# The order of seven products: TensorE's up-projection queue written by hand, and weight splits placed behind the operand turns

## The chip, the cores and the metric

The kernel runs on one core of a Trainium2 chip. The metric is the time of one execution in device microseconds (us). The core's engines work side by side, each on its own queue in order: TensorE (PE, matmuls; its weight loads are listed as PEld), VectorE (DVE), ScalarE (ACT), GpSimd (POOL), and SyncE (SP), which issues the DMAs.

## The reference

A hybrid encoder layer of width 1024 runs over a prompt of 512 tokens and a sample of 1024 tokens with shared weights. What matters here is its second half, for the sample:

```python
for l in range(DEPTH):                       # DEPTH = 1
    ...                                      # attention and convolution heads, added to x
    h = _rmsnorm(x, norm_ffn_g[l])
    u = _dwconv(h @ w_up[l], ffn_dw_w[l], ffn_dw_b[l])        # 3 taps along the tokens
    x = x + (jax.nn.silu(u[..., :D_FF]) * u[..., D_FF:]) @ w_down[l]
return _rmsnorm(x, norm_final_g)
```

`w_up` is 1024 x 5632 (a gate half and a value half of 2816 columns each), `w_down` 2816 x 1024. All numbers are 32-bit floats.

## The kernel before

**Precision.** A 32-bit operand is split into a high part that TensorE takes in its rounded 32-bit form and a low part, the rest. A product is then three matmuls: high by high, high by low, low by high (lines 1045 to 1047 of `prod`). A split is one copy on ACT (line 1031 or 970) and one subtraction on POOL or DVE (line 921, the helper `sub`; `add` is line 918).

**Stages.** The program first does projections, convolution and attention for both inputs, then the prompt's feed-forward half. From about 900 us on it does the sample's feed-forward half: the up-projection until about 1356 us and the down-projection to the end.

**The sample's up-projection.** It uses a Strassen-like scheme: a 2 x 2 block product with seven block products instead of eight. `NJ` = 22 blocks of 128 gate and 128 value columns (index `j`) are worked through, the two halves of 512 tokens side by side in a bank pair (left and right, `L` and `R`). Each block has seven products, numbered 1 to 7, each of four slices `c` by three matmuls of 128 x 128 by 128 x 512, so 84 matmuls. `A[i, c]` holds the activations' operand of product `i`, which lasts over all blocks; `ops[j, i]` holds the split weight operand of block `j`. `block_up` names quarters of a block's raw weights; `sums_up(j)` makes the weight sums that products 7, 6, 4, 5 need (one on POOL, three on DVE), and `split_up(j, i, ...)` splits the named operands. Products 1 and 2 take the raw quarters, so their splits come before the sums.

A block has two pairs of accumulator banks: `x` (gate) and `wy` (value), taken together by `pair_banks` from four such pairs. So two blocks can be under way. The products share banks:

```python
def first(j):                 # 1: into x left, then ACT copies it to wy right as a seed
    if j < NJ:
        pair_banks(j)
        s = st[j]
        prod(s["x"][:, L], j, 1, True, True)
        nc.scalar.copy(s["wy"][:, R], s["x"][:, L])          # line 1117
```

The others follow the same pattern: `second` adds product 2 to `x` left. `sixth` adds product 6 to `wy` right, and ACT copies the sum out (line 1126). `seventh` adds product 7 to `wy` right, and ACT copies the sum to `x` right as a seed (line 1135). `fourth` adds product 4 to `x` right. `fifth` puts product 5 into `wy` left, ACT copies it out (line 1146) and DVE adds it to `wy` right. `third` adds product 3 to `wy` left, and DVE adds the sum copied out by `sixth`. A product that adds to a seeded bank waits for the copy that seeds it.

`gate_part(j)` reads `x` out (ACT line 1158, two DVE taps, lines 1159 and 1160, then a tanh), `value_part(j)` does the same with `wy`, multiplies both (DVE lines 1177 and 1179) and writes to memory what the down-projection needs. Only then are the bank pairs free for block `j + 2`.

**Operand turns.** The activations' operands are rows that are scaled and summed (`scaled`, line 943, and `last_sum`), then turned by TensorE: `turned(i, get)` does four steps, each of four 128 x 128 transposes into one bank (line 968), an ACT copy and a DVE subtraction (lines 970 and 971). The last five operands (4, 6, 7, 5, 3; 20 steps) are turned during the products 2 and 4 of block 0 and 2 of block 1: `every(n, gen)` spreads n steps over the four slices of a product. The turn banks (four) are then given up, and their place becomes two more bank pairs. For blocks 0 and 1 the first products were made before these pairs exist; `armed` (line 1110) writes a dummy product into `wy` right so that later products may add to it, and ACT copies the first product over it (line 1243).

**Who orders the work.** A scheduler that simulates the engines places each instruction: those written first come first, but an engine that would be idle takes whatever is ready. Buffers are named slots (`Slots`), taken in the order in which they came free: 61 of 2048 bytes (`h`), two slightly larger (`d`), 15 of 4096 (`q`) and 4 of 4224 (`c`). `split_up` takes one `q` or `c` for both parts of an operand. `reserve` and `raws` set some `q` slots aside for raw weights (`load_up`, line 995). Inside `tc.manual_schedule(engines={...})` the named engines keep the written order. Before the change this holds for PE from the operand turns through the first blocks, and for SP from the last block on; in the loop over `j` the scheduler orders PE.

The loop body before, from line 1467 on:

```python
        split_up(j + 1, 1, 2)
        sixth(j)
        sums_up(j + 1)
        value_part(j - 1)
        second(j)
        seventh(j)
        split_up(j + 1, 6, 4)
        fifth(j)
        fourth(j)
        gate_part(j)
        ...                          # j == NJ - 1: SP by hand, load_next(10), down_step(0)
        first(j + 1)
        third(j)
        split_up(j + 1, 7, 5, 3)
```

**The down-projection** is again seven products, each over 11 pairs of blocks; `down_step(k)` is one step of 12 matmuls (lines 1346 to 1348). Its first step stands in the loop's last round.

Of the kernel before, what the change touches and what calls it, by code (L numbers as in the profile page):

```python
# [28 lines left out]
NJ = FF // P  # L29
# [67 lines left out]
def tile_hybrid_encoder(ctx: ExitStack, tc: tile.TileContext, xs, rel_bias, norm_attn_g, w_in,  # L97
# [819 lines left out]
    def add(out, a, b, eng=None):  # L917
        (eng or nc.vector).tensor_tensor(out, a, b, op=ALU.add)  # L918

    def sub(out, a, b, eng=None):  # L920
        (eng or nc.vector).tensor_tensor(out, a, b, op=ALU.subtract)  # L921
# [42 lines left out]
    def turned(i, get):  # L964
        for c in range(4):
            held, ap = get()
            for b in range(4):
                nc.tensor.transpose(ap[:, b * P:(b + 1) * P], block_rows(i, b)[:, c * P:(c + 1) * P], ident[:])
            hi, lo = A[i, c] = (sb.tile([NT], F32R), sb.tile([NT], F32R))
            nc.scalar.copy(hi[:], ap)  # L970
            sub(lo[:], ap, hi[:].bitcast(F32))
            held = None
            yield 0.0
        key = {6: "s2", 5: "s1", 7: 1, 3: 0}.get(i)
        for b in range(4):
            rows.pop((key, b), None)
# [9 lines left out]
    def reserve(n):  # L986
        for slot in [s for s in sb.free if s[0][0] == "q"][:n]:
            sb.free.remove(slot)
            raws.free.append(slot)

    def load_up(j, half):
        if j < NJ:
            r = uraw[j, half] = raws.tile([KC, P])
            col = half * FF + j * P
            nc.sync.dma_start(r[:], w_up[0][:, col:col + P].rearrange("(k p) c -> p k c", p=P))

    def block_up(j, half, k):
        return uraw[j, half][:, 4 * k:4 * k + 4, :].rearrange("p k c -> p (k c)")
# [8 lines left out]
    def sums_up(j):  # L1007
        if j < NJ:
            g0, g1, v0, v1 = (block_up(j, half, k) for half in range(2) for k in range(2))
            t = third_sum[j] = sb.tile([NT])  # L1010
            sub(t[:], v1, v0, nc.gpsimd)
            sub(v0, v0, g0)
            sub(g0, v1, v0)
            sub(g1, g1, g0)

    def split_up(j, *which, apart=False):
        if j >= NJ:
            return
        for i in which:
            if i == 7:  # L1020
                held = third_sum.pop(j)
                src = held[:]
            else:
                src = block_up(j, *{1: (0, 0), 2: (0, 1), 6: (0, 0), 4: (0, 1), 5: (1, 0), 3: (1, 1)}[i])
            if not apart and any(s[0][0] in "qc" for s in sb.free):
                t = sb.tile([2, NT], F32R)
                hi, lo = Part(t, 0), Part(t, 1)
            else:
                hi, lo = sb.tile([NT], F32R), sb.tile([NT], F32R)
            ops[j, i] = hi, lo  # L1030
            nc.scalar.copy(hi[:], src)  # L1031
            sub(lo[:], src, hi[:].bitcast(F32), nc.gpsimd)
            held = None
            done.add((j, i))
        for half, pair in ((0, (6, 4)), (1, (5, 3))):
            if (j, half) in uraw and all((j, i) in done for i in pair):
                uraw.pop((j, half))

    def prod(out, j, i, start, stop, between=None):
        whi, wlo = ops.pop((j, i))  # L1040
        go = dict(skip_group_check=not start)
        for c in range(4):
            hi, lo = A[i, c]
            s = slice(c * P, (c + 1) * P)
            nc.tensor.matmul(out, whi[:, s], hi[:], start=(start and c == 0), stop=False, **go)  # L1045
            nc.tensor.matmul(out, whi[:, s], lo[:], start=False, stop=False, **go)  # L1046
            nc.tensor.matmul(out, wlo[:, s], hi[:], start=False, stop=(stop and c == 3), **go)  # L1047
            if j == NJ - 1:
                A.pop((i, c))
            if between is not None:  # L1050
                next(between, None)
# [52 lines left out]
    def pair_banks(j):  # L1104
        st[j] = dict(x=wide(), wy=wide())

    def armed(out):

        hi, lo = A[1, 0]
        nc.tensor.matmul(out, hi[:, 0:P], hi[:], start=True, stop=True)  # L1110

    def first(j):
# [4 lines that stand above are left out]
            nc.scalar.copy(s["wy"][:, R], s["x"][:, L])  # L1117

    def second(j, between=None):
        prod(st[j]["x"][:, L], j, 2, False, True, between)  # L1120

    def sixth(j, between=None):
        s = st[j]
        s["u2"] = sb.tile([NT])
        prod(s["wy"][:, R], j, 6, False, True, between)
        nc.scalar.copy(s["u2"][:], s["wy"][:, R])

    def fourth(j, between=None, start=False):
        prod(st[j]["x"][:, R], j, 4, start, True, between)
# [11 lines left out]
    def fifth(j):  # L1141
        s = st[j]
        W, Y = s["wy"][:, L], s["wy"][:, R]
        prod(W, j, 5, True, True)
        p5 = sb.tile([NT])
        nc.scalar.copy(p5[:], W)
        add(Y, Y, p5[:])

    def third(j):
        s = st[j]  # L1150
        W = s["wy"][:, L]
        prod(W, j, 3, False, True)
        add(W, W, s.pop("u2")[:])
# [17 lines left out]
    def value_part(j):  # L1171
        if j < 0:
            return
        p = j // 2
        s = st.pop(j)
        ug, t = s["ug"], s["t"]
        nc.vector.scalar_tensor_tensor(t[:], t[:], 1.0, ug[:], op0=ALU.add, op1=ALU.mult)
        uv = dwconv(s.pop("wy"), NJ + j)
        nc.vector.tensor_tensor(t[:], t[:], uv[:], op=ALU.mult)
        del ug, uv  # L1180
        s.clear()
        if j % 2 == 0:
            even[p] = t
            nc.sync.dma_start(ga[1, p][:], t[:, L])
            return
        e, x, y = even.pop(p), sb.tile([W2]), sb.tile([NT])
        for i, blk in ((2, L), (4, R)):
            nc.sync.dma_start(ga[i, p][:], t[:, blk])
        add(x[:, R], e[:, R], t[:, R])
        sub(x[:, L], e[:, L], e[:, R], nc.gpsimd)  # L1190
        sub(e[:, R], x[:, R], e[:, L])
        sub(y[:], t[:, L], e[:, R], nc.gpsimd)
        for i, b in ((5, x[:, R]), (7, x[:, L]), (6, e[:, R]), (3, y[:])):
            nc.sync.dma_start(ga[i, p][:], b)
# [3 lines left out]
    by_hand = tc.manual_schedule(engines={mybir.EngineType.PE})  # L1198
# [6 lines left out]
    def chain(*gens):  # L1205
        for g in gens:
            yield from g

    def every(n, gen):

        for c in range(4):
            for _ in range((n * (c + 1)) // 4 - (n * c) // 4):
                next(gen, None)
            yield

    turns = chain(*(turned(i, turn_bank) for i in (4, 6, 7, 5, 3)))
# [5 lines left out]
        nc.scalar.copy(a[:], st[j]["x"][:, L])  # L1222
        firsts.append(a)
    second(0, every(7, turns))
    split_up(0, 7)
    fourth(0, every(7, turns), True)
    split_up(1, 7)
    split_up(0, 5)
    second(1, every(6, turns))
    for _ in turns:  # L1230
        raise RuntimeError("turns left")
    pt_guard.__exit__(None, None, None)
# [6 lines left out]
    def arm():  # L1239
        for j in range(2):  # L1240
            Y = st[j]["wy"][:, R]
            armed(Y)
            nc.scalar.copy(Y, firsts[j][:])
            yield

    fourth(1, chain(iter((None,)), arm()), True)
    firsts.clear()
    reserve(2)
    load_up(2, 0)
    load_up(2, 1)  # L1250
    split_up(1, 5)
    sixth(0)
    split_up(0, 3)
# [10 lines left out]
    fifth(1)  # L1264
    sums_up(2)
    third(0)
    split_up(2, 6, 4)
    value_part(0)
    first(2)
    third(1)  # L1270
    split_up(2, 7, 5, 3)
    load_up(4, 0)
    load_up(4, 1)
    by_hand.__exit__(None, None, None)


    pr, second_half = {}, {}
# [181 lines left out]
    for j in range(2, NJ):  # L1459
        for half in range(2):  # L1460
            load_up(j + 3, half)
        if j >= NJ - 3:
            sb.free.extend(raws.free)
            raws.free.clear()
        if j >= NJ - 2:
            load_next(4)
        split_up(j + 1, 1, 2)
        sixth(j)
        sums_up(j + 1)
        value_part(j - 1)  # L1470
        second(j)
        seventh(j)
        split_up(j + 1, 6, 4)
        fifth(j)
        fourth(j)
        gate_part(j)
        if j == NJ - 1:
            by_hand = tc.manual_schedule(engines={mybir.EngineType.SP})
            by_hand.__enter__()
            load_next(10)  # L1480
            down_step(0)
        first(j + 1)
        third(j)
        split_up(j + 1, 7, 5, 3)
    sb.free.extend(raws.free)
    value_part(NJ - 1)

# [70 lines left out]
```

## Time and profile before

| What | us |
|---|---|
| Median of 3 runs (lowest to highest) | 1568.78 (1568.59 to 1568.99) |
| The profiled execution, its own time | 1569.84 |
| Its span, first to last instruction | 1568.1 |
| PE busy | 1523.8 (97% of the span) |
| DVE busy | 1161.2 (74%) |
| ACT busy | 797.8 (51%) |
| POOL busy | 786.9 (50%) |

A row of a timeline reads: start, length, engine, line, operation, output<-inputs by the program's names, shapes, count, and in brackets the idle time before it and what ended it. A row of the waits reads: who waits, for what, microseconds in total, times, longest. A row of groups reads: line, engine, operation, names, shapes, count, then busy time, mean nanoseconds of one, and idle time before. A row of stretches gives the length and then, for PE, weight loads, DVE, ACT and POOL, the busy time and count, then TensorE's granted clock, the DMA share and GB/s. Matmuls overlap, so their pace is read from their starts and not from their recorded lengths.

### The profile page before, as it was taken

The numbers are of one execution on the slowest core, as the hardware profiler recorded it, in microseconds if no ns is written. First come the engines' busy times: TensorE is split into PE (matmuls) and PEld (weight loads), VectorE is DVE, ScalarE is ACT, GpSimd is POOL, SyncE is SP. The second block draws the span as 40 slices with busy tenths as digits, with TensorE's granted clock in tenths as the row PEclk, the third lists the DMA queues.
The fourth block names the chain that finished last, engine by engine and source line by source line (L and its number), as shares of the span: only waits on it lengthen the run. The fifth ranks groups of instructions, "written<-read, shape, count | busy, mean of one in ns | idle before, by whom it ended". The sixth has DMA issues, their size and how long they took to land.

```text
span 1568.1 us, 20174 instructions
## 1 busy us (share of the span) xinstructions
PE 1523.8 (97%) x6909; PEld 1238.2 (79%) x6909; DVE 1161.2 (74%) x1687; ACT 797.8 (51%) x1426; POOL 786.9 (50%) x603
## 2 busy tenths in 40 slices
PE   8999999999998999999999999999999999999998
PEld 6787788887887778888877878777777778888886
DVE  7999868638988996756675858576766676877795
ACT  4634565335565655655554355454545445454364
POOL 7651344238575676656652337575757566000225
PEclk9999999999999999999999999999999999999999
DMA  7573246446332333333656222323232332594642
GB/s 228 158 199 95 86 120 162 128 138 164 108 115 62 107 108 108 107 96 98 213 182 198 81 68 78 110 93 109 88 114 89 108 101 98 176 383 149 221 142 108
DMA packets 209771, 207.62 MB, mean 132 GB/s; under 512 B 11156, under 2 KB 150748, under 8 KB 209541
## 3 DMA queue, kind: packets, MB, share of 16 engines
q1 hardware_dynamic: 209669, 206.35, 41.9%
q8 instruction: 54, 0.88, 0.2%
q14 instruction: 48, 0.39, 0.1%
HBM read 158.84 MB, written 48.51 MB: 132 GB/s over the span
## 4 chain that ended last, share of the span: by engine, by line
PE 77%; DVE 10%; DMA 4%; issue 3%; POOL 3%; ACT 2%; SPq 0%; POOLq 0%; ACTq 0%; DVEq 0%
PE w L1045 8%; PE w L1047 8%; PE w L1046 8%; PE w L1347 5%; PE w L1346 5%; PE w L1348 5%; PE u L250 4%; PE u L251 4%; PE u L253 4%; DVE c L293 3%; PE b L253 3%; PE b L250 3%; PE b L251 3%; PE u L641 2%; PE u L642 2%
## 5 line engine op out<-in xcount | busy, mean ns | idle before, releaser
L144 POOL TENSOR_TENSOR q<-q,q 128x1024 fp32r<-128x1024 f32 x72 | 174.9, 2434 | 70.1 <-ACT q L143 32.0
L1045 PE MATMUL w<-h,q 128*128 128x512 f32 x470 | 185.4, 396 | 4.6 <-ACT w L1135 2.6
L921 POOL TENSOR_TENSOR q<-q,q 128x512 fp32r<-128x512 f32 x101 | 143.1, 1429 | 91.8 <-ACT q L1031 91.7
L1047 PE MATMUL w<-h,q 128*128 128x512 f32 x470 | 184.4, 392 | 0.0
L1046 PE MATMUL w<-h,q 128*128 128x512 f32 x448 | 175.7, 392 | 0.0
L250 PE MATMUL u<-h,q 128*128 128x512 f32 x400 | 159.9, 400 | 3.6 <-DVE h L775 2.8
L251 PE MATMUL u<-h,q 128*128 128x512 f32 x400 | 159.5, 399 | 0.6 <-DVE h L212 0.6
L253 PE MATMUL u<-h,q 128*128 128x512 f32 x384 | 152.1, 396 | 2.1 <-POOL q L144 2.1
L293 DVE SCALAR_TENSOR_TENSOR c<-c,cvw,c 128x512 f32<-128x512 f32 x184 | 138.1, 750 | 2.4
L143 ACT CAST q<-q 128x1024 fp32r<-128x1024 f32 x72 | 75.6, 1049 | 78.8 <-POOL q L144 45.5
L1045 PEld LDWEIGHTS w<-h,q 128*128 128x128 f32 x470 | 88.2, 188 | 27.6 <-ACT w L1135 4.4
L1047 PEld LDWEIGHTS w<-h,q 128*128 128x128 f32 x470 | 88.2, 188 | 20.5
L250 PE MATMUL b<-h,q 128*128 128x512 f32 x256 | 102.1, 399 | 1.7 <-DVE d L323 1.7
L1346 PE MATMUL w<-h,h 128*128 128x512 f32 x264 | 103.6, 392 | 0.0
L1348 PE MATMUL w<-h,h 128*128 128x512 f32 x264 | 103.6, 392 | 0.0
L921 DVE TENSOR_TENSOR h<-h,h 128x512 fp32r<-128x512 f32 (+1 forms) x128 | 92.7, 766 | 11.4 <-ACT h L925 8.8
L251 PE MATMUL b<-h,q 128*128 128x512 f32 x256 | 100.6, 393 | 0.0
L253 PE MATMUL b<-h,q 128*128 128x512 f32 x256 | 100.6, 393 | 0.0
L1046 PEld LDWEIGHTS w<-h,q 128*128 128x128 f32 x448 | 84.1, 188 | 18.5
L918 POOL TENSOR_TENSOR q<-q,q 128x1024 f32<-128x1024 f32 x8 | 23.8, 2985 | 146.4 <-DVE q L918 135.6
L1347 PE MATMUL w<-h,h 128*128 128x512 f32 x244 | 95.9, 393 | 0.0
L250 PEld LDWEIGHTS u<-h,q 128*128 128x128 f32 x400 | 76.4, 191 | 20.8 <-DVE h L775 3.3
(452 smaller groups left out, 4099.3 us busy)
## 6 DMA issues: line engine op xcount, KB each, us to landing
q<-in_w_up SPq DMA_DIRECT2D x88, 512.0 KB
h<-in_w_down SPq DMA_DIRECT2D x90, 256.0 KB
ga<-q SPq DMA_DIRECT2D x64, 256.0 KB
h<-ga SPq DMA_DIRECT2D x57, 256.0 KB
q<-in_w_in SPq DMA_DIRECT2D x28, 512.0 KB
q<-in_x_sample SPq DMA_DIRECT2D x15, 512.0 KB
h<-qsd SPq DMA_DIRECT2D x24, 256.0 KB
q<-ga SPq DMA_DIRECT2D x20, 256.0 KB
```

What stands on the lines that cost most here:

```text
L144: (nc.vector if dve else nc.gpsimd).tensor_tensor(lo[:], raw[:], hi[:].bitcast(F32), op=ALU.subtract)
L250: nc.tensor.matmul(out, whi[:, kc, :], hi[:], start=(kc == 0), stop=False)
L251: nc.tensor.matmul(out, whi[:, kc, :], lo[:], start=False, stop=False)
L253: nc.tensor.matmul(out, wlo[:, kc, :], hi[:], start=False, stop=(kc == KC - 1))
L293: nc.vector.scalar_tensor_tensor(acc[:], src(t), w(t), acc[:], op0=ALU.mult, op1=ALU.add)
L921: (eng or nc.vector).tensor_tensor(out, a, b, op=ALU.subtract)
L1045: nc.tensor.matmul(out, whi[:, s], hi[:], start=(start and c == 0), stop=False, **go)
L1046: nc.tensor.matmul(out, whi[:, s], lo[:], start=False, stop=False, **go)
L1047: nc.tensor.matmul(out, wlo[:, s], hi[:], start=False, stop=(stop and c == 3), **go)
L1346: nc.tensor.matmul(out, sh[:, c], th[:], start=(p == 0), stop=False)
L1347: nc.tensor.matmul(out, sh[:, c], tl[:], start=False, stop=False)
L1348: nc.tensor.matmul(out, sl[:, c], th[:], start=False, stop=(p == NPAIR - 1))
```

## The change

PE's hand order no longer ends before the loop but covers the whole up-projection, and from the last block on a second one covers SP and PE to the end of the kernel. In the loop the products are written in another order: second, seventh, first of the next block, fifth, fourth, sixth of the next block, third. The splits of operands 7, 5 and 4 move to other places in the round. In the prologue the splits of operand 7 of blocks 0 and 1 and of operand 5 of block 0 stand behind the turns, the last turns are spread as eight steps over four slices, so they end one slice earlier, and the arming of the two banks comes one slice later.

```diff
@@ -1222,11 +1222,8 @@
     second(0, every(7, turns))
-    split_up(0, 7)
     fourth(0, every(7, turns), True)
-    split_up(1, 7)
-    split_up(0, 5)
-    second(1, every(6, turns))
+    second(1, chain(every(8, turns)))
     for _ in turns:
         raise RuntimeError("turns left")
@@ -1243,11 +1240,14 @@
-    fourth(1, chain(iter((None,)), arm()), True)
+    fourth(1, chain(iter((None, None)), arm()), True)
     firsts.clear()
+    split_up(0, 7)
+    split_up(1, 7)
     reserve(2)
     load_up(2, 0)
     load_up(2, 1)
+    split_up(0, 5)
     split_up(1, 5)
     sixth(0)
     split_up(0, 3)
@@ -1264,14 +1264,14 @@
     fifth(1)
     sums_up(2)
     third(0)
-    split_up(2, 6, 4)
+    split_up(2, 6)
     value_part(0)
     first(2)
     third(1)
-    split_up(2, 7, 5, 3)
+    split_up(2, 7, 5, 4, 3)
     load_up(4, 0)
     load_up(4, 1)
-    by_hand.__exit__(None, None, None)
+    sixth(2)
@@ -1465,23 +1465,26 @@
         split_up(j + 1, 1, 2)
-        sixth(j)
+        second(j)
         sums_up(j + 1)
         value_part(j - 1)
-        second(j)
         seventh(j)
-        split_up(j + 1, 6, 4)
+        split_up(j + 1, 6)
+        first(j + 1)
         fifth(j)
+        split_up(j + 1, 7, 5)
         fourth(j)
         gate_part(j)
-        if j == NJ - 1:
-            by_hand = tc.manual_schedule(engines={mybir.EngineType.SP})
+        if j < NJ - 1:
+            sixth(j + 1)
+        else:
+            by_hand.__exit__(None, None, None)
+            by_hand = tc.manual_schedule(engines={mybir.EngineType.SP, mybir.EngineType.PE})
             by_hand.__enter__()
             load_next(10)
             down_step(0)
-        first(j + 1)
         third(j)
-        split_up(j + 1, 7, 5, 3)
+        split_up(j + 1, 4, 3)
```

## The prediction

> **What bounds the kernel now.** I read the page's busy shares first, then TensorE's waits from 900 us on, then its timeline at each wait, and last the other engines' timelines beside them.
>
> ```profile
> PE 1523.8 (97%) x6909; PEld 1238.2 (79%) x6909; DVE 1161.2 (74%) x1687; ACT 797.8 (51%) x1426; POOL 786.9 (50%) x603
> PE w L1045 <- ACT w L1135: 2.6, 4, 0.7
> PE t L968 <- DVE h L921: 2.0, 1, 2.0
> PE w L1045 <- ACT w L1117: 1.9, 4, 0.5
> PE w L1110 <- DVE q L921: 1.4, 1, 1.4
> 1039.30:1118.50 79.20, 78.03 (x337) 62.91 (x336) 52.63 (x49) 38.50 (x57) 51.46 (x37) 1.00 0.31 100
> 1356.00:1568.10 212.10, 205.08 (x890) 166.78 (x889) 157.68 (x212) 97.85 (x178) 44.20 (x39) 0.99 0.57 195
> ```
>
> The first row says that TensorE (PE) is the bound. The next four are all that TensorE waited for between 900 and 1360 us, the stretch that the change touches: recorded idle time, times, longest. Nothing else there can be gained. The two last rows are stretches (length, then busy time of PE, weight loads, DVE, ACT, POOL, then clock): four blocks of the up-projection's loop, and the down-projection.
>
> What a wait costs is read from the starts of the matmuls, since their recorded ends overlap the next.
>
> ```profile
> 1045.05 0.40 PE L1045 MATMUL w<-h,q 128*128 128x512 f32 x1
> 1045.28 0.40 PE L1046 MATMUL w<-h,q 128*128 128x512 f32 x1
> 1045.52 0.40 PE L1047 MATMUL w<-h,q 128*128 128x512 f32 x1
> 1046.58 0.50 PE L1045 MATMUL w<-h,q 128*128 128x512 f32 x1 [0.66 <-ACT w L1135]
> 1046.91 0.39 PE L1046 MATMUL w<-h,q 128*128 128x512 f32 x1
> ```
>
> Undisturbed matmuls start 0.23 us apart, so a product of 12 takes 2.76 us and a block of 84 takes 19.3 us. Here one start comes after 1.06 us and the next after 0.33: 0.83 + 0.10 = 0.93 us lost, 0.27 more than the 0.66 recorded as idle. For the loop's eight waits that is 2.6 + 1.9 + 8 x 0.27 = 6.7 us. The stretch of four blocks agrees: 336 matmuls would take 77.3 of its 79.2 us, and the 1.9 us left over holds two waits.
>
> **The loop (6.7 us at stake).** Both waits are a product that sits too close behind the ACT copy which seeds its bank. At 1046.58 the fourth product comes straight after the seventh, whose sum ACT must first copy (L1135). In the other kind the sixth waits for the first product's copy (L1117), and that copy waits for something itself:
>
> ```profile
> L1117 ACT COPY w<-w x20: 570/570/590, 955.2 to 1323.3; 128x512 f32<-128x512 f32 x20
>   DVE q L1160: 11.1, 8
> L918 DVE TENSOR_TENSOR w<-w,h 128x512 f32<-128x512 f32 x39 | 27.2, 696 | 37.4 <-ACT h L1146 30.1 <-PE w L1047 7.3
> L1158 ACT ACTIVATE q<-w,vecs,fw 128x1024 f32<-128x1024 f32 x40 | 48.3, 1208 | 28.7 <-PE w L1047 25.3 <-DVE w L918 2.4 <-DMA ga<-q 0.6
> L1160 DVE SCALAR_TENSOR_TENSOR q<-w,fw,q 128x1023 f32<-128x1023 f32 x39 | 49.8, 1278 | 0.7
> L921 POOL TENSOR_TENSOR q<-q,q 128x512 fp32r<-128x512 f32 x89 | 125.4, 1422 | 68.7 <-ACT q L1031 68.7
> ```
>
> The second row, from the idle times of L1117, says what the copy waited for: the last depthwise tap of the value part two blocks back, which still reads the bank pair that the copy writes.
>
> In the new hand order each block runs second, seventh, first of the next block, fifth, fourth, sixth of the next block, third. Seventh to fourth, first to sixth and fifth to third then each have two other products between them: 5.5 us for a copy of 0.57. The long chain starts where the third product ends: DVE's add 0.70, ACT's 1.21, two taps of 1.28, together 4.5 us. The sixth of the next block starts five products later (second, seventh, first, fifth, fourth: 13.8 us), so after the copy some 8.7 us are left for what DVE has queued ahead: three sums and one 1024-wide operation, about 4 us by the 0.70 row and the 1.28 row. I count both kinds of wait gone.
>
> The operand splits lose cover. A split is a copy on ACT (0.57, as L1117's of the same size) and a subtraction of 1.42 on POOL. The next block's first operand is now written two products (5.5 us) ahead of its use, where it was five; two splits take 2 x 1.42 + 0.57 = 3.4 us, and they may run earlier than written, since the new order holds at most seven operand pairs at once where the old held eight, which leaves a slot more. Fourth's split moves behind the third product: it keeps the raw half-block a little longer, and the load into that place is needed two blocks (38 us) later, against a landing time like this one of an equal 512 KB load:
>
> ```profile
> 90.48 4.08 DMA q<-in_w_in
> ```
>
> So the loads cost nothing. If one split is late now and then I allow 0.5 us: 6.7 - 0.5 = 6.2 us gained.
>
> **The operand turns (3.9 us at stake).**
>
> ```profile
> 908.23 0.48 PE L1045 MATMUL w<-h,q 128*128 128x512 f32 x1
> 909.22 0.27 PE L968 MATMUL t<-ident,c 128*128 128x128 f32 x1
> 909.33 0.27 PE L968 MATMUL t<-ident,q 128*128 128x128 f32 x1
> 911.65 0.66 PE L968 MATMUL t<-ident,h 128*128 128x128 f32 x4 [2.04 <-DVE h L921]
> 917.94 0.48 PE L1045 MATMUL w<-h,h 128*128 128x512 f32 x1
> 919.51 0.48 PE L1045 MATMUL w<-h,h 128*128 128x512 f32 x1
> 912.00:914.00 2.00, 2.00 (x11) 1.72 (x10) 1.98 (x4) 0.59 (x1) 0.00 (x0) 0.66 0.00 0
> 914.00:916.00 2.00, 2.00 (x9) 1.60 (x8) 1.16 (x2) 1.17 (x2) 0.00 (x0) 0.50 0.04 8
> ```
>
> Three products and two turns take 1.57 us when nothing waits (917.94 to 919.51), and a turn of four transposes 0.11 apart is 0.43. From 908.23 to 917.94 lie twelve products and seven turns: 4 x 1.57 - 0.43 = 5.85 us, but 9.71 passed. Of the 3.9 us lost, 2.0 is the wait, and the rest the granted clock, which fell to 0.66 and 0.50 behind it (2 x 0.34 + 2 x 0.50 = 1.7 us).
>
> ```profile
> 897.55 1.40 DVE L943 SCALAR_TENSOR_TENSOR c<-q,rs,q 128x512 f32<-128x512 f32 x2
> 903.73 2.44 DVE L943 SCALAR_TENSOR_TENSOR q<-c,rs,q 128x512 f32<-128x512 f32 x2 [1.53 <-POOL rs L128]
> 907.55 1.77 DVE L921 TENSOR_TENSOR q<-q,q 128x512 f32<-128x512 f32 x1
> 909.36 1.63 DVE L921 TENSOR_TENSOR q<-q,h 128x512 f32<-128x512 f32 x1
> 910.91 3.07 DVE L921 TENSOR_TENSOR h<-t,h 128x512 fp32r<-128x512 f32 x5
> 904.23 1.40 POOL L921 TENSOR_TENSOR q<-h,q 128x512 fp32r<-128x512 f32 x1 [0.53 <-ACT q L1031]
> 906.99 1.78 POOL L921 TENSOR_TENSOR q<-h,q 128x512 fp32r<-128x512 f32 x1 [1.36 <-ACT q L1031]
> 908.73 1.71 POOL L921 TENSOR_TENSOR q<-q,q 128x512 fp32r<-128x512 f32 x1
> ```
>
> The transposes at 911.65 need a turn bank that DVE frees with its first subtraction at 910.91. DVE is late because its row sums run beside three POOL subtractions, which are the splits that the change moves: 2.44 instead of 1.40 for the pair, 1.77 and 1.63 instead of the 0.70 of the add's row, 3.0 us in all. Without them the subtraction starts near 907.9 and no transpose waits. Written behind the turns they could still run early, as ACT and POOL take what is ready. But the two third sums now hold their small slots through the turns, so the last turned operands overflow into the large slots that those splits had, and the splits are left with slots that come free only when a turned row is done. If only the third of the three moves away, 0.9 us is gained; if all, 3.9; if the moved splits meet another DVE sum of 0.70, up to 1 us comes back. I take 3.2, near the upper end, since the slots speak for it.
>
> [...]
>
> **The armed banks (1.6 us at stake).**
>
> ```profile
> 927.16 1.18 ACT L1031 CAST q<-q 128x512 fp32r<-128x512 f32 x2
> 928.20 0.62 ACT L970 CAST d<-t 128x512 fp32r<-128x512 f32 x1
> 927.86 0.40 PE L1047 MATMUL w<-h,h 128*128 128x512 f32 x1
> 929.61 0.50 PE L1110 MATMUL w<-h 128*128 128x512 f32 x1 [1.35 <-DVE q L921]
> 930.14 0.59 ACT L1243 COPY w<-h 128x512 f32<-128x512 f32 x1 [1.31 <-PE w L1110]
> ```
>
> The arming matmul writes where the turn banks lay and waits until the last turn is read out, whose ACT copy stands behind two splits. It starts 1.75 us after its forerunner instead of 0.23, and the next start is 0.1 late as before: 1.6 us lost. The change ends the turns three matmuls earlier in second(1) and arms three matmuls later in fourth(1): 6 x 0.23 = 1.4 us, so 0.2 remains, or nothing if the splits have left ACT. New is that the sixth follows the second arming matmul at once. The first bank's copy ends 930.73, 1.12 us after its arming matmul; the sixth starts five matmuls (1.15 us) after it: 0 to 0.1, or 0.6 with a split ahead on ACT. Net 1.4 us gained, between 0.8 and 1.6.
>
> **The down-projection.** Its order is now by hand too. The page shows no wait for TensorE in its 212 us, and 77 steps of 12 matmuls at 0.23 are 212.5 us, so an order cannot gain. It can lose at the seam, where the first down step comes behind fourth(21), one product of the loop before the end, and seventh(21) has only one product between itself and fourth(21), 2.76 us for a 0.57 copy: 0 to 0.5 us, taken as 0.2.
>
> **Sum.** 6.2 + 3.2 + 1.4 - 0.2 = 10.6 us of the profiled execution's 1569.8, so 1559.2. That execution is 1.1 us above the median of the runs, and the median becomes 1558.2. If everything is gained (6.7 + 3.9 + 1.6) it is 1556.6; with each stage's lower end (4 in the loop, 0.9, 0.8) and 0.5 lost at the seam 5.2 is gained: 1563.6. A measurement of this kernel can tell about 0.2%, 3.1 us, from no change. Chance of this case 0.64.
>
> **Rivals.** First, the loop's waits come back elsewhere: DVE and POOL are busy 52.6 and 51.5 of 79.2 us, so taps can finish late and the wait moves to another product of the hand order, at about its old size. Then only turns and arming gain, 4.4 us: 1564.4. Against it: each pair has 5.5 us. Chance 0.11.
>
> Second, the gain is given back: the down steps' operands are not ready sooner (DVE is busy 157.7 of 212 us), and TensorE waits there for what it has won. 1568.8 at worst. Against it: no wait is seen there, and the splits would have to be late at once. Chance 0.08.
>
> Third, slower: first of the next block waits for its operand in every block. If its split starts only with second(j), and POOL has two other subtractions ahead (2 x 1.42), the operand is ready 2 x 1.42 + 3.4 = 6.2 us later against 5.5, and with POOL slowed to 1.75 as beside DVE above 7.6: a wait of 0.7 to 2.1 us in each of 19 blocks, 13 to 40 us, less the 10.6: 1571 to 1598, for one number 1580. It decides from 0.56 us a block on, where the gain is eaten. A fixed order also cannot put another product into the hole, as a free one can. For it: POOL is busy in 65% of the loop. Against it: today no TensorE wait in the loop is for POOL, and one slot more is free. Chance 0.17.
>
> The range takes in the forecast's ends and the first two rivals, and a little of the third: 1556.0 to 1571.0, which leaves out most of the third and about 0.03 below. Faster by over 0.2% (below 1565.7): 0.64 and most of the first rival, 0.73. Within: 0.09. Slower: 0.18.
>
> **What would show it.** Right: the waits of TensorE hold neither L1135 nor L1117 in the loop, four blocks take about 77.4 us, the rows of DVE at 903 to 911 are 0.7 us each with no POOL subtraction beside them, the clock stays at 1.00 through the turns, and the arming matmul waits under 0.3 us. Wrong: a wait of TensorE for a POOL or ACT split (L921, L1031's result) once per block, POOL subtractions still beside the row sums, or a new wait in the down-projection's stretch.

## The result, and the profile after

The changed kernel takes 1630.32 us (median of 6 runs, 1626.43 to 1634.58), the kernel before 1568.16 us beside it. The ratio is 1.0399, with a 95% interval of 1.0378 to 1.0420: 62 us slower, where 10.6 us faster was forecast.

TensorE's waits in the changed kernel, from 890 us to the end (its span is 1629.8 us):

```profile
PE w L1045 <- ACT q L1031: 25.9, 8, 5.1
PE w L1047 <- POOL q L921: 21.6, 9, 3.7
PE w L1045 <- ACT w L1135: 0.9, 1, 0.9
```

The waits that the change was to remove are gone. Of the waits for seeding copies (L1117, L1135) one of 0.9 us is left, at the end of the loop. In their place stand 47.5 us of a kind that the kernel before did not have: a product waits for the high part of its weight operand (ACT's split, L1031) and then for the low part (POOL's subtraction, L921).

From one seventh product to the next both orders run one full block of products, so the first and last start of its copy (L1135) measure the loop. Before, and in the changed kernel:

```profile
L1135 ACT COPY w<-w x20: 570/570/582, 965.0 to 1341.0; 128x512 f32<-128x512 f32 x20
L1135 ACT COPY w<-w x20: 570/570/578, 959.2 to 1401.7; 128x512 f32<-128x512 f32 x20
```

The first is 5.8 us earlier and the last 60.7 us later: the preparation of blocks 0 and 1 gained, and the 19 blocks between took 442.5 us instead of 376.0. The preparation, as it was forecast (a stretch of the turns, then VectorE's and TensorE's timelines):

```profile
914.00:916.00 2.00, 2.00 (x16) 1.78 (x15) 1.70 (x3) 1.50 (x4) 0.13 (x1) 1.00 0.01 4
```

```profile
902.96 1.42 DVE L943 SCALAR_TENSOR_TENSOR q<-c,rs,q 128x512 f32<-128x512 f32 x2 [1.53 <-POOL rs L128]
905.75 0.68 DVE L921 TENSOR_TENSOR q<-q,q 128x512 f32<-128x512 f32 x1
924.36 0.50 PE L1110 MATMUL w<-h 128*128 128x512 f32 x1 [0.25 <-DVE q L921]
```

The row sums take 1.42 and 0.68 us instead of 2.44 and 1.77, no transpose waits, the clock stays at 1.00, and the arming matmul waits 0.25 us instead of 1.35.

Now the loop. Four of its blocks as one stretch (before, 79.2 us at a clock of 1.00), and one stall in TensorE's timeline:

```profile
1038.97:1132.40 93.43, 83.55 (x340) 66.32 (x339) 58.15 (x49) 39.04 (x58) 49.61 (x38) 0.93 0.26 85
```

```profile
1066.53 0.79 PE L1045 MATMUL w<-h,q 128*128 128x512 f32 x1 [2.68 <-ACT q L1031]
...
1069.75 0.79 PE L1047 MATMUL w<-h,q 128*128 128x512 f32 x1 [2.00 <-POOL q L921]
1070.34 0.63 PE L1045 MATMUL w<-h,q 128*128 128x512 f32 x1
1070.76 0.63 PE L1046 MATMUL w<-h,q 128*128 128x512 f32 x1
```

The product is the sixth of block 7. It stalls twice, once for each part of its operand, and behind the stall the matmuls start 0.43 us apart and not 0.23, until 1073 (granted clock 0.51 from 1069.75 on). This comes once in two blocks, nine times, at the sixth product of an odd block (the last time for the low part alone). The other engines ahead of it:

```profile
1056.25 1.29 POOL L921 TENSOR_TENSOR h<-q 128x512 f32<-128x512 f32 x1 [2.91 <-DMA q<-in_w_up]
1057.58 1.76 DVE L921 TENSOR_TENSOR q<-q,q 128x512 f32<-128x512 f32 x1 [0.91 <-POOL h L921]
1059.27 1.21 DVE L1179 TENSOR_TENSOR c<-c,c 128x1024 f32<-128x1024 f32 x1
...
1061.24 1.81 DVE L921 TENSOR_TENSOR q<-q,q 128x512 f32<-128x512 f32 x1
1063.08 0.32 SPq L1194 DMA_DIRECT2D ga<-q  x1
1063.13 1.65 POOL L921 TENSOR_TENSOR h<-c,q 128x512 f32<-128x512 f32 x1 [0.63 <-DVE q L921]
1064.82 0.62 ACT L1031 CAST c<-q 128x512 fp32r<-128x512 f32 x1 [3.11 <-POOL h L921]
1065.34 0.61 ACT L1031 CAST q<-h 128x512 fp32r<-128x512 f32 x1
1065.86 0.61 ACT L1031 CAST q<-q 128x512 fp32r<-128x512 f32 x1
1067.96 1.73 POOL L921 TENSOR_TENSOR q<-q,q 128x512 fp32r<-128x512 f32 x1
```

Read it from below. The low part of the sixth operand is written from 1067.96, its high part from 1065.86, both into one large slot (`q`). In the compiled program the data that lay in this slot before belong to the pair of value parts of blocks 4 and 5: VectorE wrote them at 1061.24, the DMA issued at 1063.08 stores them for the down-projection, and the copy waits for that store. In the trace the store's last semaphore step comes at 1065.07. So the place was free only 0.8 us before the copy started. These 0.8 us are ACT's queue: the copy is third, behind the splits of block 8's second and block 7's seventh operand, and the first of these waited 3.11 us for another slot of the same pair (`c`, line 1179), which POOL still read (1063.13). The subtraction of the low part loses another 1.5 us behind those of the same two operands on POOL.

The pair is late in its turn: ahead of VectorE's product at 1059.27 stands a weight sum of block 9 (1057.58), which waits for POOL's sum (1056.25) and that for a load. So a split waits for a slot that the down-projection's data still fill.

All nine stalls read like this. In the odd blocks from 3 to 19 the sixth operand takes a slot that line 1194 stores from, and its copy starts 0.1 to 2.0 us after that store is done, 0.7 or 0.8 us ahead of the product. In the even blocks from 4 to 20 the slot was left by line 1177, and the copy runs 10 to 19 us ahead. The written order shows why: `value_part(j - 1)` stands two calls ahead of `split_up(j + 1, 6)`, and for an odd block the slot that the pair has just left is the next to be taken.

Who is short of slots shows in the copies of the operand turns, by the slot that they write (groups of L970; the first row is of before, the others of after):

```profile
L970 ACT CAST h<-t x19: 578/587/621, 907.3 to 926.7; 128x512 fp32r<-128x512 f32 x19
L970 ACT CAST h<-t x18: 572/587/596, 906.1 to 919.9; 128x512 fp32r<-128x512 f32 x18
L970 ACT CAST q<-t x1: 586/586/586, 923.0 to 923.0; 128x512 fp32r<-128x512 f32 x1
```

One high part has moved from a small slot to a large one, and a low part with it: in the compiled programs the 56 parts of the activations' operands lie in 53 small, 2 middle and 1 large slot before, and in 51, 2 and 3 after. The third sums of blocks 0 and 1 sit in the small slots while the last turns run, because their splits now come later. The activations' operands live to the last block, so the loop has two large slots fewer, and two small ones more, which a split takes only where no large one is free when it is written.

### The profile page after: what moved, and what is told of

It is laid out like the page before. It is cut to its first block, busy times and chain, and to the rows that moved or that the text cites. A ratio compares the mean times of both kernels' runs of the same rounds, so it can differ in the third digit from the quotient of the medians.

```text
span 1629.8 us, 20191 instructions
## 1 busy us (share of the span) xinstructions
PE 1543.8 (95%) x6909; PEld 1250.9 (77%) x6909; DVE 1174.9 (72%) x1687; ACT 799.6 (49%) x1426; POOL 778.9 (48%) x603
## 5 line engine op out<-in xcount | busy, mean ns | idle before, releaser
L1045 PE MATMUL w<-h,q 128*128 128x512 f32 x406 | 168.6, 415 | 26.9 <-ACT q L1031 25.9
L1047 PE MATMUL w<-h,q 128*128 128x512 f32 x406 | 168.6, 415 | 21.6 <-POOL q L921 21.6
L921 POOL TENSOR_TENSOR q<-q,q 128x512 fp32r<-128x512 f32 x90 | 123.9, 1384 | 133.4 <-ACT q L1031 133.1
L1046 PE MATMUL w<-h,q 128*128 128x512 f32 x384 | 157.9, 411 | 0.0
L1045 PEld LDWEIGHTS w<-h,q 128*128 128x128 f32 x406 | 81.4, 200 | 48.6 <-ACT q L1031 29.3
L1047 PEld LDWEIGHTS w<-h,q 128*128 128x128 f32 x406 | 80.8, 199 | 45.2 <-POOL q L921 26.7
L143 ACT CAST q<-q 128x1024 fp32r<-128x1024 f32 x72 | 75.5, 1049 | 79.2 <-POOL q L144 45.0
L921 DVE TENSOR_TENSOR h<-h,h 128x512 fp32r<-128x512 f32 (+1 forms) x128 | 92.1, 762 | 11.2 <-ACT h L925 9.3
L1046 PEld LDWEIGHTS w<-h,q 128*128 128x128 f32 x384 | 77.0, 200 | 17.3
```

## The experiments

Theory S is this shortage. Rival O is the new order itself, which leaves the sixth operand too little time; rival H is the weight sums that stand ahead of the value part and wait for late loads (they are written there in the old loop too). The first four runs set them against each other: they give the slots back, take each half of the change alone, and take two slots from the kernel before.

**Two slots given back.**

```diff
     split_up(1, 7)
+    for key, pair in A.items():
...
+            for x in pair:
+                if x.slot[0][0] == "q" and len(sb_h()) > 0 and moved[0] < 2:
+                    n = sb.tile([NT], F32R, among="h")
+                    nc.scalar.copy(n[:], x[:])
...
     reserve(2)
```

`sb_h()` lists the free small slots, and `moved[0]` counts the copies; the copy takes the part's place in `A`.

> The changed kernel with two copies added on ScalarE, right behind the moved third-sum splits of blocks 0 and 1: the two turned activation operands beyond the first that lie in large slots are copied into the small slots that the third sums have just left, so that the loop gets back the two large slots that it has in the kernel before. Nothing else is changed. Theory S (the loop is short of two large slots, so that the split of the sixth operand waits for the store of the value pair): the waits of L1045 for ScalarE's copies (25.9 us) and of L1047 for POOL's subtractions (21.6 us) fall under 5 us together, and the time is 1556 to 1565. Rival O (the new order of the products leaves the sixth operand too little time, whatever slots there are): 1620 to 1632. Rival H (the sums of the next block stand ahead of the value part on VectorE and POOL and wait for late loads): 1615 to 1632.

Measured: 1568.04 us, ratio 0.9984 (0.9972 to 0.9995). Its waits of TensorE over the same stretch:

```profile
PE w L1363 <- DVE h L921: 2.5, 1, 2.5
PE w L1045 <- ACT w L1135: 2.2, 2, 2.0
PE w L1047 <- POOL q L921: 1.3, 1, 1.3
```

By the ratios, two copies remove 65 us (0.0415 of 1570). The order of products and of the sums is as in the changed kernel, so O and H fall as causes of their own. The total misses the expectation by 3 us; the first two rows, which lie in the down-projection (line 1363 here is line 1347 before) and, but for 0.2 us, at the loop's end, are taken up below.

**The loop alone.** The preparation of before, the loop body of after.

```diff
     load_up(4, 0)
     load_up(4, 1)
-    by_hand.__exit__(None, None, None)
+    sixth(2)
...
```

> The kernel before with the changed loop alone: its own preparation of blocks 0 and 1 (operand turns in sevens, splits in their old places), and from there the new order of the seven products and TensorE's order by hand to the end of the loop. Theory S: the activations' operands keep their one large slot, so the loop doesn't wait: about 5 us of the preparation's gain are missing, 1560 to 1568. Rival O: the loop's loss in full and no gain ahead of it, 1630 to 1638. Rival H: the same, 1625 to 1638.

Measured: 1568.67 us, ratio 0.9984 (0.9971 to 0.9996). No stall in the loop; 0.7 us beyond the slower end of what S expected.

**The preparation alone.** The reverse: the changed preparation, then `by_hand.__exit__` and the old loop.

> The changed preparation of blocks 0 and 1 (turns in eights, splits behind them) with the loop of the kernel before, its order of products and its scheduling. Theory S: the old loop also has two large slots fewer; it has its own slack, which the trace of before does not give in one number, so 1570 to 1630, and new waits of TensorE for splits in the loop. Rivals O and H: the loop runs as before and the 5 us won by 948 us stay: 1561 to 1566.

Measured: 1565.60 us, ratio 0.9973 (0.9963 to 0.9982). This is what O and H expected, and S in its plain form is wrong here: with the same two slots missing the old loop does not stall, and the preparation's gain of 4 us stays. Neither half of the change is slow by itself; only the two together are. TensorE's rows show only 1.3 us of waits in this loop, but the rest has moved to the rows of its weight loads (PEld: 4.9 us in 9 waits for L1117). Counted from the starts of the matmuls, 0.231 us apart when nothing waits, 5.5 us are lost between 957 and 1330 us, against 6.8 before.

**Two slots taken from the kernel before.**

```diff
     load_up(2, 1)
+    kept = [sb.tile([W2]) for _ in range(2)]
...
+        if j == NJ - 3:
+            kept.clear()
```

> The kernel before with two more large slots held and never used, from the start of the loads of block 2 until three blocks ahead of the end of the loop. Theory S: slower than before, 1575 to 1630, with TensorE waiting for splits in every second block. Rivals O and H: the number of slots is not what decides, 1567 to 1572.

Measured: 1574.94 us, ratio 1.0032 (1.0022 to 1.0043): 5 us slower, just under the lowest edge of S, and without the waits for splits that S named: no such wait is among TensorE's rows. The old order does well enough with two large slots fewer. S needs a second half: the new order can't spare them.

The next four runs test that, and how it depends on the number of slots and on the place of the sixth product.

**The new loop with two slots held.** The loop alone, as above, and `kept` as above.

> The kernel before with the changed loop alone, as in the run before it, and two large slots held unused from the start of the loads of block 2 until three blocks ahead of the end of the loop. Theory S in its second form (the new order needs the two slots, the old order hardly: holding them cost the old loop 4.7 us): the stall of every second block comes back, some nine waits of ScalarE's split and nine of POOL's, 25 and 20 us, and with the half clock behind them 1615 to 1635. A rival: the loss in the changed kernel came from something else of its preparation (the splits of the operands 5 and 7 moved behind the turns), and the slots only removed a symptom: 1566 to 1585.

Measured: 1622.28 us, ratio 1.0336 (1.0321 to 1.0352), against 0.9984 without the hold. Waits:

```profile
PE w L1047 <- POOL q L921: 26.2, 9, 3.5
PE w L1045 <- ACT q L1031: 9.2, 9, 2.3
```

That is 55 us between the two ratios. The stall is back, nine times, without any of the changed preparation, so the moved splits need no other way than the slots to do their harm. Here most of the wait is for the low part, whose subtraction stands behind others on POOL. POOL waits for no load of weights in this kernel, while in the changed kernel it waited 44.6 us in 12 waits for them: late loads lengthen the stall there, but it doesn't need them.

**One slot given back.**

```diff
-                if x.slot[0][0] == "q" and len(sb_h()) > 0 and moved[0] < 2:
+                if x.slot[0][0] == "q" and len(sb_h()) > 0 and moved[0] < 1:
```

> As the changed kernel with the two copies, but with one copy alone, so that the loop has one large slot fewer than the kernel before. If each missing slot pushes the ring of slots by the same share, half of the 62 us: about 1600. If the ring has slack for one (the split of the sixth operand then takes a slot that a matmul has left and not one that a store has left): 1566 to 1572, and if one missing slot is as bad as two, 1615 to 1632. I take the middle, 1590, with 1566 to 1632 for the range.

Measured: 1570.77 us, ratio 1.0013 (0.9997 to 1.0029). My middle of 1590 was wrong: by the ratios the first missing slot costs 4.6 us against the run with both given back (0.0029 of 1570; the two intervals all but touch), the second 60 (0.0386). It is a cliff, as the slots explain: from block 5 on the sixth operand takes other slots here, and its copy runs about 4 us ahead of the product.

**The sixth product one place later.**

```diff
-        if j < NJ - 1:
-            sixth(j + 1)
-        else:
+        if j == NJ - 1:
...
         third(j)
+        if j < NJ - 1:
+            sixth(j + 1)
```

> The changed kernel, its two slots short as it is, with one edit: the product of the sixth operand of the next block stands behind the third product of this block and not ahead of it, as in the old order, so that its split has one more product (12 matmuls at 0.228 us, 2.74 us) of cover. Theory S: the waits of ScalarE (2.5 to 5.1 us each, nine of them) shrink by 2.7 us each, those of POOL behind them stay at 1.7 to 2.5 us until they overlap with the first, so 9 x 2.7 = 24 us and some half-clock time less: 1595 to 1608. If the stall is a cycle, in which the store, the slot and the split follow TensorE around, a later use moves everything with it and nothing is won: 1620 to 1632.

Measured: 1593.95 us, ratio 1.0160 (1.0143 to 1.0177), one microsecond below the range.

```profile
PE w L1045 <- DVE w L918: 13.1, 15, 1.1
PE w L1047 <- POOL q L921: 11.3, 9, 2.1
PE w L1045 <- ACT q L1031: 1.0, 1, 1.0
```

The edit takes 38 us off (profiled spans of 1629.8 and 1591.8), but not in the parts that were reckoned. The waits for the sixth operand fall from 47.5 us to 12.3, so by 35 us and not 24 (the expectation counted nine waits for ACT where there were eight). The first row is the edit's price: the third product has lost the sixth as cover and waits 15 times for VectorE's add behind the fifth. That the balance, 23 us, lies near the 24 reckoned is luck. The rest is the clock, which the expectation only called "some": starts that come late by under 0.6 us add up to 21.4 us in the changed kernel between 957 and 1398 us and to 4.8 here, and four blocks here ran at a granted clock of 1.00 instead of 0.93. The stall does not follow TensorE around.

**Slots given back, TensorE's hand order ended in the last block.**

```diff
-            by_hand = tc.manual_schedule(engines={mybir.EngineType.SP, mybir.EngineType.PE})
+            by_hand = tc.manual_schedule(engines={mybir.EngineType.SP})
```

> The changed kernel with the two copies, and TensorE's order by hand ended ahead of the last block's third product, where the kernel before also leaves the rest to the scheduler. In the run with the two copies and the order by hand to the end, TensorE waited 2.03 us for ScalarE's copy of the fifth product at this seam (1336.88 us) and ran the ten products behind it at 0.427 us each, 2.0 us more; and 2.5 us for VectorE at 1516.80. If the hand order of the down-projection is what costs this, the time is 2 to 6.5 us below the 1568.0 of that run: 1561.5 to 1566. If the seam waits anyway: 1567 to 1569.

Measured: 1566.77 us, ratio 0.9985 (0.9974 to 0.9995), the same ratio as with the order by hand to the end; the time lies between the two expectations. The copy that the expectation names is that of the seventh's sum (L1135); it is the fifth product that waits for it. The seam's wait fell to 0.2 us, and the down-projection held 3.5 us of waits for VectorE instead of 2.5.

The last four: the one operand, the scheduler, and the part of the change that starts it.

**Two small slots for the sixth operand.**

```diff
-        split_up(j + 1, 6)
+        split_up(j + 1, 6, apart=True)
```

> The changed kernel with one argument more in the loop: the split of the sixth operand takes two small slots and not one large one (the two small ones that the third sums left and that nothing uses). The activations stay in their three large slots, so the loop is short of two large slots as in the changed kernel, and nothing else is edited. Theory S, narrowed to this operand: the stall came from the slot that this one split got, which the store of the value pair held; its copy now follows the second operand's on ScalarE without a wait for a store, so the waits for ScalarE's splits fall under 3 us and those for POOL's under 6 us together: 1558 to 1568. If any operand that is short of a slot stalls TensorE (the fifth and seventh still wait for the store): 1580 to 1620. Rival H (the sums ahead of the value part): 1615 to 1632.

Measured: 1562.76 us, ratio 0.9946 (0.9929 to 0.9963). TensorE's longest wait from 890 us on, and ACT's row of waits ahead of splits into a `c` slot (960 to 1340 us):

```profile
PE w L1045 <- ACT w L1135: 2.8, 1, 2.8
```

```profile
ACT c L1031 <- issue: 22.9, 8, 3.6
```

In the changed kernel that row of ACT was:

```profile
ACT c L1031 <- POOL h L921: 24.6, 8, 3.2
```

A ScalarE split into a `c` slot still waits, as often and nearly as long. (`issue` says that the profile names no releaser; in the compiled program these eight wait for VectorE's product of the value part, line 1179, and start 0.1 us after it.) The shortage of slots is the same. But the sixth operand takes no slot of the pair any more. Its split and its product in block 7:

```profile
1027.66 0.62 ACT L1031 CAST h<-q 128x512 fp32r<-128x512 f32 x1 [2.17 <-DVE q L921]
1047.24 0.40 PE L1045 MATMUL w<-h,h 128*128 128x512 f32 x1
```

The copy runs 19.6 us ahead of its use, into a small slot that had been free for 9 us. The edit also moved the copy in ACT's queue, but at the stall shown above the queues account for 0.8 us on ACT and 1.5 on POOL, and the copy could not have started before the store was done.

The same line divides all kernels of this case. In the four that stall at the sixth product (the changed one, the new loop with two slots held, the sixth one place later, and the free order below) the sixth operand of every odd block from 3 to 19 takes a slot that line 1194 stores from, and its copy starts 0.0 to 2.0 us after that store. In the others the slot was left by something else, but for two blocks of the kernel with one slot given back, and the copy runs 3 us or more ahead of the product.

**The same, with TensorE's hand order ended in the last block.**

> The same with TensorE's order by hand ended in the last block and not at the end of the down-projection. In the kernel with the copies this took 2 us of waits from the seam and gave as much back later in the down-projection (ratios 0.9984 and 0.9985): I expect the same here, within 1.5 us of the run before this one, 1557 to 1569; 2 to 4 us faster if the seam's wait of 2.0 to 2.6 us isn't answered by a later one.

Measured: 1561.90 us, ratio 0.9937 (0.9925 to 0.9949). The intervals of the two overlap, so the seam's share is not settled by them; both beat both kernels. Of 1568.78 us this ratio makes 1558.9, where the prediction had 1558.2; that they meet so closely is in part luck, since this kernel has two edits more than the change. Four blocks of its loop, in which TensorE never idles:

```profile
1024.37:1101.90 77.53, 77.53 (x338) 63.07 (x337) 55.10 (x49) 37.94 (x56) 48.98 (x37) 1.00 0.32 102
```

**The scheduler orders TensorE in the loop.** The changed kernel with `by_hand.__exit__` ahead of `sixth(2)`, and SP alone by hand from the last block on.

> The changed kernel with the order by hand ended ahead of the loop, so that the scheduler may set TensorE's order in the new loop, in the same two slots too few. Theory S: the slots still run through the stores, but where the sixth operand is late the scheduler puts other products ahead of it, so most of the stall is filled: 1568 to 1595. If the scheduler can't fill it (it runs out of operands as well): 1610 to 1632. If the order by hand was of no weight: 1627 to 1633.

Measured: 1587.84 us, ratio 1.0106 (1.0093 to 1.0119).

```profile
PE w L1047 <- POOL q L921: 15.3, 8, 2.0
```

With the order free the waits for the high part fall from 25.9 to 0.7 us, those for the low part stay at 15.3. By the ratios the fixed order, nearly all of it in the loop (the last block alone changed nothing above), made 46 us of the loss; with a free one the changed kernel would still be 17 us slower than before.

**The two seventh operands split in their old places.**

```diff
     second(0, every(7, turns))
+    split_up(0, 7)
     fourth(0, every(7, turns), True)
+    split_up(1, 7)
...
-    split_up(0, 7)
-    split_up(1, 7)
     reserve(2)
```

> The changed kernel with one part undone: the splits of the seventh operands of blocks 0 and 1 stand in their old places among the operand turns (the split of block 0's fifth operand stays behind them). The third sums leave their small slots there, so the last turned operands find small slots, and the activations hold one large slot as in the kernel before; no copies are added. Theory S: no stall in the loop, as with the copies, and part of the turns' gain is given back since two POOL subtractions stand beside VectorE's row sums again (wait of the transposes 0.5 to 2 us): 1565 to 1571. If the stall needs nothing of the splits' place: 1620 to 1632.

Measured: 1563.17 us, ratio 0.9961 (0.9945 to 0.9978), 2 us below the expectation: the transposes waited 0.4 us and not 0.5 to 2. Undoing this one part of the change removes the stall, so the move of these two splits is what set the loop short.

## Why the prediction was wrong

**The turns and the armed banks: right.** 3.2 + 1.4 us were forecast. From the start of the second product of block 0 to that of its sixth TensorE took 25.96 us before (905.61 to 931.57) and 20.83 with the preparation alone (906.87 to 927.70): 5.1 us gained; that run as a whole gained 4.2 (0.9973 of 1570.24). The signs named for it came: the clock at 1.00, an arming wait under 0.3, and row sums of 0.7 us, but for one of 0.78 in the changed kernel, beside a POOL subtraction (906.18) that had not moved away.

**The failing step: the price of the splits that lose cover, 0.5 us "if one split is late now and then", on the ground that "the new order holds at most seven operand pairs at once where the old held eight, which leaves a slot more".** The step counted what the loop asks for and not what it has. In the turns the other half was in hand: "the last turned operands overflow into the large slots". There it served as a reason for a gain and was not followed to how long those operands live, which is to the last block. Put together, the loop had two large slots fewer, and the sixth operand of every odd block got a slot that a store still held. The runs showed 47.5 us of waits for it, and 19 blocks 66 us longer; the new loop with two slots held lost 55 us against the new loop without, the old one 5.

**The cover of the splits.** It was worked out for the first operand, at five products before and two after, but not for the sixth, whose use also moved one product forward. Giving that one product back takes 38 us off.

**The slower rival** had the kind of mechanism: a product waits for its operand behind other subtractions on POOL, and a fixed order cannot fill the hole. That is true of the low part here. It had the wrong operand, no slot in it, and 1571 to 1598 for a price. The range ended at 1571, the foot of that rival. "Today no TensorE wait in the loop is for POOL" was said against it; that was true of before and said nothing of a loop with other memory.

**The loop's 6.2 us: right, once the slots are there.** In the kernels with two small slots for the sixth operand no wait for L1117 or L1135 is left inside the loop, and four blocks take 77.5 us, where 77.4 was named. Counted from the starts, 6.8 us were lost between 957 and 1330 us before and 0.1 are with the end freed.

**The seam: mis-sized.** The step took 0.2 us, at most 0.5. In the kernels whose loop does not stall and whose order is by hand to the end the wait there is 1.4 to 2.8 us. In the kernel with small slots, ACT and TensorE at the seam:

```profile
1330.49 1.20 ACT L1158 ACTIVATE q<-w,vecs,fw 128x1024 f32<-128x1024 f32 x1
...
1333.66 0.58 ACT L1135 COPY w<-w 128x512 f32<-128x512 f32 x1
1334.29 0.50 PE L1045 MATMUL w<-h,q 128*128 128x512 f32 x1 [2.78 <-ACT w L1135]
```

The seeding copy is short, but it stands behind the reading-out of a bank pair and four splits of the down-projection's operands. The prediction priced the copy and left out its queue. It also had the wrong product: the one that waits is the fifth, which writes the bank pair that the copy reads, and not the fourth.

**The down-projection** gave something back in the three kernels with copied parts: a wait of 2.5 us for VectorE with two copies (at 1516.80) and with one (at 1514.78), and 3.5 us with the order freed at the end. No other kernel of which the loop does not stall waits there for more than 0.3 us. In those three VectorE's two last residual adds stand back to back beside POOL's, as the last section shows; why the copies bring the scheduler to this order was not tried.

## What to carry to other kernels

Where buffers are slots taken in the order in which they come free, moving an instruction moves allocations too: for each value that the edit makes live longer, ask which value is pushed into the next size of slot, and how long that one lives. Two missing slots cost 5 us at most under one order and 60 under another, so a changed order and changed memory have to be priced together; one missing slot cost 5 us here and two cost 65. When a product stalls for an operand, ask what lay before in the slot that its split writes, and who must still read that: here a store. Then look at what stands ahead of it in the queues. Giving the one urgent operand other slots was worth at least as much as giving back both.

## What the runs showed of the hardware

**The clock falls behind some waits of 2 to 3 us and not behind others.** Two kernels at the seam, the loop alone (first two rows) and the one with two copies (last two):

```profile
1335.60 0.50 PE L1045 MATMUL w<-h,q 128*128 128x512 f32 x1 [2.63 <-ACT w L1135]
1335.60:1340.00 4.40, 4.40 (x19) 3.65 (x20) 4.40 (x8) 3.70 (x7) 0.00 (x0) 1.00 0.00 0
```

```profile
1336.88 0.50 PE L1045 MATMUL w<-h,q 128*128 128x512 f32 x1 [2.03 <-ACT w L1135]
1336.90:1341.00 4.10, 4.10 (x11) 3.26 (x12) 4.10 (x6) 2.17 (x4) 0.00 (x0) 0.58 0.00 0
```

After the longer wait, of 2.63 us, the clock stayed at 1.00; after the shorter, of 2.03, it was 0.58, and eight matmuls from 1337.74 to 1340.73 started 0.43 us apart. So in these rows the length of a wait alone does not decide; what else does was not shown.

**VectorE beside GpSimd.** In the kernel before, at the down-projection's residual adds (spans on POOL are rough):

```profile
1500.97 1.22 DVE L918 TENSOR_TENSOR q<-w,q 128x1024 f32<-128x1024 f32 x1
1503.80 2.88 DVE L921 TENSOR_TENSOR h<-h,h 128x512 fp32r<-128x512 f32 x1
1506.60 3.43 DVE L918 TENSOR_TENSOR q<-q,q 128x1024 f32<-128x1024 f32 x1
1512.75 1.21 DVE L918 TENSOR_TENSOR q<-q,q 128x1024 f32<-128x1024 f32 x1
1513.88 0.68 DVE L921 TENSOR_TENSOR h<-h,h 128x512 fp32r<-128x512 f32 x1
1500.54 11.74 POOL L918 TENSOR_TENSOR q<-q,q 128x1024 f32<-128x1024 f32 x4 [10.87 <-DVE q L918]
```

While POOL runs four adds of 2.9 us, VectorE's add of the same size takes 3.43 us, and 1.21 once POOL is done; a subtraction of half the size takes 2.88 and then 0.68. The add at 1500.97, of which one input is a bank of TensorE's, runs beside POOL too and takes 1.22. In the kernel with two copies both adds fall beside POOL, and the wait of 2.5 us named above lies right behind:

```profile
1508.17 6.77 DVE L918 TENSOR_TENSOR q<-q,q 128x1024 f32<-128x1024 f32 x2
```
